# A gated recurrence: root of 1 - a^2 rewritten with a tanh of the half, its square on GpSimd removed

## The chip, the core and the metric

One core of a Trainium2 chip runs one program. Its engines have a queue of instructions each: TensorE (PE, matmuls), VectorE (DVE), ScalarE (ACT), GpSimd (POOL) and SyncE (SP, which issues transfers). The time is the device time of one execution in microseconds (us); the kernel before took 2144.94 us, the median of three runs (2142.59 to 2145.22).

## What is computed

One block of a diffusion model over 2048 tokens of 1024 features. A token mixer has three branches: a gated linear recurrence in both directions over 512 features, a pooling branch and a gated MLP; a feed-forward part with a 3x3 convolution follows and takes most of the time. The change is in the coefficients of the recurrence:

```python
r = sigmoid(block_diag(xh, w_a, b_a))
i = sigmoid(block_diag(xh, w_x, b_x))
log_a = -LRU_C * r * softplus(-lam)
a = exp(log_a)
bterm = sqrt(-expm1(2.0 * log_a)) * (i * xf)
# then h[t] = a[t] * h[t-1] + bterm[t], forwards and backwards
```

The factor of `i * xf` is the root of 1 - a^2.

## The kernel before, in words

The features of the recurrence are four tiles of 128 (`j`), the tokens four chunks of 512 (`n`), and there are two directions (`d`). A unit (`lru_units`, written `f` or `b` in the list `ORDER`) works on one direction, one chunk and two tiles `j`; there are 8 forward units and then 8 backward ones. Ahead of them two context groups (`lru_ctx`, `c`) run the same steps on 256 context tokens, for two `j` and both directions at once, to give the first states.

A unit runs these steps for each of its two `j`. `coeffs` (L451): two matmuls into PSUM give the gates, then ScalarE takes the sigmoid of both (tiles `r` and `i`) and `t = tanh(k * r)`, where `k` is a column of `klam`, -8 times a softplus computed once by `lam_consts`; this tanh is that of log a itself. `coeffs2` (L465): ScalarE overwrites `r` by `a = exp(k * r)`; then `combine` (L471) lets GpSimd compute the square `q = r * r` (L473) and `i = i * xa` (L474), and VectorE the sum-and-product `t = (q + 1) * t` (L475). With tanh(x) = (e^2x - 1) / (e^2x + 1) that is a^2 - 1. `coeffs3` (L477): ScalarE takes the root of -t, and `finish_b` (L483) has GpSimd multiply `i` by it (L485). `scan` (L487, L491) is one VectorE instruction along the tokens; then the last state is kept (L526), and the result goes to memory (forwards) or is added to the forward result by GpSimd (`join`, L535).

All activations of ScalarE that need a table go through `act` (line 135 in the profile). It counts sigmoid and tanh as one set of functions, exp, sqrt, gelu and silu as sets of their own, and makes every instruction of a set follow those of the set before in the order of the program; a table is loaded at each change of set. So a unit has three loads: sigmoid and tanh, exp, sqrt. Other activations (identity, copy, square) may stand anywhere.

The tiles of a unit come from a pool of two (`lru_tile`), so a unit's sigmoids wait until the unit before has given its tile back. Beside the units, the same stretch of the program holds the matmuls of the input projection (`xa`, `gt`, `pl`, `uv`), the gating MLP (`gmlp`: L629 to L647, with `guv` on VectorE, `sp` and `tp` on TensorE), the pooling branch (`pool_br`: L561 to L592, with `pz`, `pa`, `pb` on VectorE and `pp` on TensorE), the modulation vectors (L672, VectorE) and the preparation of weights (L153, L271, L272, VectorE). `ORDER` gives the order in which these pieces are written; the order within each engine's queue is planned from it when the program is built, by priority and estimated durations, and each queue then runs strictly in that order. The stretch ends where the output projection starts (`wo`), at about 544 us. The feed-forward part (L376 to L378 `up`, L1023 and L1066 to L1068) follows to the end.

Of the kernel before, what the change touches and what calls it, by code (L numbers as in the profile page):

```python
# [11 lines left out]
AF = mybir.ActivationFunctionType  # L12
OP = mybir.AluOpType
# [4 lines left out]
LC = 256  # L18
CH = 512
# [49 lines left out]
def block_kernel(ctx: ExitStack, tc: tile.TileContext, x, xT, ctx_d, ctxT, cc, crow, cols_d, wm01, bm01, wmT,  # L69
                 win, wuv, gw, pw, wsT, gnorm, wout, wup, wdn, ident_d, out):  # L70
    nc = tc.nc
    V, A, G, T, S = nc.vector, nc.scalar, nc.gpsimd, nc.tensor, nc.sync
# [16 lines left out]
    def bank(tag, name):  # L89
        return banks["open"].tile([128, CH], F32, tag=tag, bufs=banks[tag], name=name)  # L90
# [24 lines left out]
    def col(name, i=0, n=1):  # L115
        return cols[:, OFF[name] + i:OFF[name] + i + n]
# [16 lines left out]
    def act(out_, in_, func, **kw):  # L133

        ins = A.activation(out_, in_, func, **kw).ins  # L135
        if SETS[func] != runs["set"]:
            runs.update(set=SETS[func], prev=runs["cur"], cur=[])
        for p in runs["prev"]:
            tc.add_manual_dep(ins, p.name, mybir.DependencyInfo(
                mybir.DependencyClass.NoSync, mybir.DependencyReason.DATA), reason="table set")  # L140
        runs["cur"].append(ins)
# [26 lines left out]
    Y = [ymix.tile([128, 4, CH], F32, name=f"Y{n}") for n in range(2)]  # L168
# [7 lines left out]
    def lru_tile(shape, dt, name):  # L176
        return mix.tile(shape, dt, tag="lru", bufs=2, name=name)
# [220 lines left out]
    klam = const.tile([128, 8], F32, name="klam")  # L398

    def lam_consts():  # L400
        e = small.tile([128, 8], F32, tag="l0", bufs=1, name="lam_e")
        y = small.tile([128, 8], F32, tag="l1", bufs=1, name="lam_y")
        y2 = small.tile([128, 8], F32, tag="l2", bufs=1, name="lam_y2")
        p = small.tile([128, 8], F32, tag="l3", bufs=1, name="lam_p")
        lam = col("lam", 0, 8)
        base = small.tile([128, 8], F32, tag="l4", bufs=1, name="lam_b")
        V.memset(base, 2.718281828459045)
        V.tensor_scalar(y, lam, -1.0, None, op0=OP.mult)
        V.tensor_tensor(e, lam, y, op=OP.min)
        G.tensor_tensor(e, base, e, op=OP.pow)  # L410
        V.tensor_scalar(y, e, 2.0, None, op0=OP.add)
        V.reciprocal(y, y)
        V.tensor_tensor(y, e, y, op=OP.mult)
        V.tensor_tensor(y2, y, y, op=OP.mult)
        V.tensor_scalar(p, y2, 1.0 / 17, 1.0 / 15, op0=OP.mult, op1=OP.add)
        for d in (13, 11, 9, 7, 5, 3, 1):
            V.tensor_tensor(p, p, y2, op=OP.mult)
            V.tensor_scalar(p, p, 1.0 / d, None, op0=OP.add)
        V.scalar_tensor_tensor(p, p, 2.0, y, op0=OP.mult, op1=OP.mult)
        V.tensor_scalar(y, lam, -1.0, 0.0, op0=OP.mult, op1=OP.max)  # L420
        V.tensor_tensor(p, p, y, op=OP.add)
        V.tensor_scalar(klam, p, -8.0, None, op0=OP.mult)


    halo = const.tile([128, 4, 2], F32, name="halo")
# [24 lines left out]
    state = const.tile([128, 4, 2], F32, name="state")  # L450

    def coeffs(j, d, xa, w, c=None, bank=None):
        bank = pB if bank is None else bank
        rp, ip = bank("rp"), bank("ip")
        T.matmul(rp[:, :w], gwt[:, j, 2 * d, :], xa, start=True, stop=True)  # L455
        T.matmul(ip[:, :w], gwt[:, j, 2 * d + 1, :], xa, start=True, stop=True)
        c = lru_tile([128, 4, CH], F32, "lru") if c is None else c
        r, i, t, q = (c[:, a, :] for a in range(4))
        act(r[:, :w], rp[:, :w], AF.Sigmoid, bias=col("ba", 4 * d + j))
        act(i[:, :w], ip[:, :w], AF.Sigmoid, bias=col("bx", 4 * d + j))  # L460
        k = klam[:, 4 * d + j:4 * d + j + 1]
        act(t[:, :w], r[:, :w], AF.Tanh, scale=k)
        return r, i, t, q, k

    def coeffs2(cs, xas, w):  # L465
        for c in cs:
            act(c[0][:, :w], c[0][:, :w], AF.Exp, scale=c[4])
        for c, xa in zip(cs, xas):
            combine(c, xa, w)

    def combine(c, xa, w):  # L471
        r, i, t, q, k = c
        G.tensor_tensor(q[:, :w], r[:, :w], r[:, :w], op=OP.mult)  # L473
        G.tensor_tensor(i[:, :w], i[:, :w], xa, op=OP.mult)  # L474
        V.scalar_tensor_tensor(t[:, :w], q[:, :w], 1.0, t[:, :w], op0=OP.add, op1=OP.mult)  # L475

    def coeffs3(cs, w):  # L477
        for c in cs:
            act(c[2][:, :w], c[2][:, :w], AF.Sqrt, scale=-1.0)
        for c in cs:  # L480
            finish_b(c, w)

    def finish_b(c, w):  # L483
        i, t = c[1], c[2]
        G.tensor_tensor(i[:, :w], i[:, :w], t[:, :w], op=OP.mult)  # L485

    def scan(o, c, w, init, rev):  # L487
        r, i = c[0][:, :w], c[1][:, :w]
        if rev:
            o, r, i = o[:, ::-1], r[:, ::-1], i[:, ::-1]  # L490
        V.tensor_tensor_scan(o, r, i, init, op0=OP.mult, op1=OP.add)  # L491

    xac = []
# [10 lines left out]
    def lru_ctx(js):  # L504
        jd = [(j, d) for j in js for d in range(2)]
        ts = [lru_tile([128, 4, CH], F32, "lrc") for j in js]
        cs = [coeffs(j, d, xac[0][:, j, :], LC, ts[j - js[0]][:, :, d * LC:(d + 1) * LC]) for j, d in jd]
        coeffs2(cs, [xac[0][:, j, :] for j, d in jd], LC)
        coeffs3(cs, LC)
        for (j, d), c in zip(jd, cs):  # L510
            q = c[3]
            scan(q, c, LC, 0.0, d == 1)
            e = LC - 1 if d == 0 else 0
            V.tensor_copy(state[:, j, d:d + 1], q[:, e:e + 1])
# [2 lines left out]

    def lru_units(d, n, js, sink):
        cs = [coeffs(j, d, Y[n][:, j, :], CH, bank=b) for j, b in zip(js, (pB, pA))]
        coeffs2(cs, [Y[n][:, j, :] for j in js], CH)  # L520
        coeffs3(cs, CH)
        for j, c in zip(js, cs):
            o = c[3]
            scan(o, c, CH, state[:, j, d:d + 1], d == 1)
            e = CH - 1 if d == 0 else 0
            V.tensor_copy(state[:, j, d:d + 1], o[:, e:e + 1])  # L526
            sink(j, n, o)
# [9 lines left out]
    def fwd(n, js):  # L537
        lru_units(0, n, js, keep_f)

    def bwd(n, js):  # L540
        lru_units(1, n, js, join)
# [198 lines left out]
    prep_uv([conv0])  # L740
    set_inv(10)
    lam_consts()

    def xstats(n):
# [29 lines left out]
    def preps():  # L774
# [8 lines left out]
    run = {  # L783
        "x": lambda n: xnext(int(n)),
        "c": lambda j: lru_ctx(J[j]),
        "a": lambda n, j: xa(int(n), J[j]),
        "f": lambda n, j: fwd(int(n), J[j]),
# [155 lines left out]
    for i in range(len(tiles) + 2):  # L943
        if i < len(tiles):
            n, tt = tiles[i]
# [165 lines left out]
    for c in range(NP + 1):  # L1111
        if c < NP:
            gi, i = divmod(c, GRP)
# [11 lines left out]
        for s in range(8):  # L1125
# [10 lines left out]
            if s % 4 == 3 and c > 0 and c % GRP == 0:  # L1136
                q = s // 4
# [108 lines left out]
```

## Time and profile before

| | |
|---|---|
| median of three runs | 2144.94 us |
| profiled execution | 2143.54 us |
| its span, first to last instruction | 2141.8 us |
| TensorE busy | 2006.3 us (94%) |
| VectorE busy | 1586.2 us (74%) |
| ScalarE busy | 1194.2 us (56%) |
| GpSimd busy | 611.9 us (29%) |
| mean granted TensorE clock | 0.969 |
| table loads on ScalarE | 77, 98.8 us |

The busy shares are averages over the whole span, most of which is the feed-forward part. A row of the timeline gives the start, the duration and the instruction with its tiles (output<-inputs) and shapes; in brackets stands how long the engine had been idle before it and what ended that. "x2" in a timeline are two instructions in a row, with the time from the start of the first to the end of the last. A row of the waits says who waited for whom: total, number of times, longest. All ScalarE activations with a table have the helper's line, L135.

### The profile page before, as it was taken

The page shows a single profiled execution, that of the slowest core. Times are in us where ns is not written, and L with a number is a line of the kernel's source. Part 1 is how long each engine was busy: PE and PEld are TensorE (multiplying, and loading weights), DVE is VectorE, ACT ScalarE, POOL GpSimd, SP SyncE. Part 2 cuts the span into 40 slices and gives each one's busy share as a digit, 9 for nine tenths or more (in the row PEclk, how much of TensorE's full clock was granted, in tenths as well). Part 3 has the DMA queues.
Part 4 walks back from the last instruction along what each step waited for, and adds up shares of the span by engine and source line. Part 5 has one row for each costly group of instructions (what it writes and reads, how often), then busy time and mean ns, then how long its engine had stood idle before and what let it go on. Part 6 is the DMA issues. An engine that isn't in the chain of part 4 may idle for free.

```text
span 2141.8 us, 24253 instructions
## 1 busy us (share of the span) xinstructions
PE 2006.3 (94%) x9203; PEld 930.4 (43%) x9203; DVE 1586.2 (74%) x2212; ACT 1194.2 (56%) x1665; POOL 611.9 (29%) x457
## 2 busy tenths in 40 slices
PE   5878989798899998999999999999999999999995
PEld 1433444343455543444444444444444444444442
DVE  5787778999565259978767776867777686777876
ACT  4776755455255446656565555645556465555453
POOL 2332334445256411101121121112212121221156
PEclk8989999899999999999999999999999999999998
DMA  8421243412333110315455464545545454454238
GB/s 339 181 99 47 69 153 113 158 40 93 134 133 128 60 64 20 138 68 124 89 122 95 79 132 73 101 83 104 90 88 106 71 103 88 101 94 68 40 157 157
DMA packets 74564, 225.03 MB, mean 105 GB/s; under 512 B 8400, under 2 KB 19024, under 8 KB 69584
## 3 DMA queue, kind: packets, MB, share of 16 engines
q0 software_dynamic: 21312, 77.60, 21.5%
q1 hardware_dynamic: 53136, 145.89, 19.7%
q8 instruction: 72, 1.18, 0.2%
q14 instruction: 44, 0.36, 0.1%
HBM read 120.70 MB, written 102.76 MB: 104 GB/s over the span
## 4 chain that ended last, share of the span: by engine, by line
PE 54%; DVE 5%; POOL 1%; ACT 1%; issue 1%; DMA 0%; POOLq 0%; SPq 0%; DVEq 0%; ACTq 0%
PE up L376 12%; PE up L378 12%; PE up L377 12%; PE dn L1066 6%; PE dn L1068 6%; PE dn L1067 6%; DVE cv L1023 3%; DVE hT L1098 0%; POOL hT L1081 0%; DVE hT L1072 0%; DMA wm<-in_wmT_dram 0%; DVE g L1031 0%; POOL fms L159 0%; PE sct L121 0%; POOL out_dram L1099 0%
## 5 line engine op out<-in xcount | busy, mean ns | idle before, releaser
L1023 DVE SCALAR_TENSOR_TENSOR cv<-z,cols,cv 128x1008 f32<-128x1008 f32 (+3 forms) x704 | 870.4, 1250 | 274.8 <-ACT cv L1017 187.0
L376 PE MATMUL up<-hT,uw 128*128 128x512 f16 x1408 | 534.3, 379 | 2.4 <-ACT z L858 2.4
L377 PE MATMUL up<-hT,uw 128*128 128x512 f16 x1408 | 534.2, 379 | 0.0
L378 PE MATMUL up<-hT,uw 128*128 128x512 f16 x1408 | 534.1, 379 | 0.0
L1083 POOL DMA_DIRECT2D accd<-dd x132 | 114.2, 865 | 701.0 <-ACT dd L1077 694.8
L858 ACT ACTIVATE z<-up,upinv 128x512 f32<-128x512 f32 x176 | 120.5, 684 | 308.9 <-PE up L378 308.5
L1077 ACT ACTIVATE dd<-dn,gdi 128x512 f32<-128x512 f32 x320 | 214.1, 680 | 112.9 <-PE dn L1068 106.4
L1066 PE MATMUL dn<-dw,gs 128*128 128x512 f16 x704 | 266.6, 379 | 5.4 <-ACT dd L1077 3.6
L1067 PE MATMUL dn<-dw,gs 128*128 128x512 f16 x704 | 266.7, 379 | 0.0
L1068 PE MATMUL dn<-dw,gs 128*128 128x512 f16 x704 | 265.1, 379 | 0.0
L376 PEld LDWEIGHTS <-uw 128*128 128x128 f16 x1408 | 139.1, 99 | 164.5 <-issue 0.6
L377 PEld LDWEIGHTS <-uw 128*128 128x128 f16 x1408 | 137.9, 98 | 167.2 <-issue 3.4
L378 PEld LDWEIGHTS <-uw 128*128 128x128 f16 x1408 | 137.9, 98 | 166.6 <-issue 0.8
L844 POOL TENSOR_TENSOR uw<-ur,uw 128x2048 f16<-128x2048 f32 x22 | 89.5, 4069 | 169.2 <-ACT ur L843 169.2
L135 ACT ACT_TABLE_LOAD x77 | 98.8, 1283 | 53.8 <-PE rp L455 24.2
L1017 ACT ACTIVATE cv<-z,cols 128x1024 f32<-128x1024 f32 x88 | 106.0, 1206 | 2.0
L1066 PEld LDWEIGHTS <-gs 128*128 128x128 f16 x704 | 72.1, 102 | 78.3
L1067 PEld LDWEIGHTS <-gs 128*128 128x128 f16 x704 | 68.7, 98 | 84.7 <-issue 7.0
L1068 PEld LDWEIGHTS <-gs 128*128 128x128 f16 x704 | 68.8, 98 | 83.1
L998 POOL TENSOR_TENSOR dw<-dr,dw 128x1024 f16<-128x1024 f32 x22 | 46.5, 2128 | 141.8 <-PE dn L1068 100.4
L150 ACT ACTIVATE junk<-g 128x1024 bf16<-128x1024 f32 x44 | 46.3, 1053 | 58.9 <-DVE g L1031 58.8
L890 PE MATMUL wo<-wo,ysp 128*128 128x512 f16 x256 | 77.6, 385 | 1.0 <-ACT gm L819 1.0
(303 smaller groups left out, 3052.9 us busy)
## 6 DMA issues: line engine op xcount, KB each, us to landing
accd<-dd POOLq DMA_DIRECT2D x132, 512.0 KB, 5.1
ur<-in_wup_dram SPq DMA_DIRECT2D x22, 1024.0 KB, 5.5
wm<-in_wmT_dram SPq DMA_DIRECT2D x64, 256.0 KB, 2.9
dr<-in_wdn_dram SPq DMA_DIRECT2D x22, 512.0 KB, 4.8
hT<-in_wm_dram SPq DMA_DIRECT2D x8, 1024.0 KB, 11.7
xt<-in_xT_dram SPq DMA_DIRECT2D x8, 1024.0 KB, 7.1
ro<-in_wout_dram SPq DMA_DIRECT2D x16, 512.0 KB, 3.5
xr<-in_x_dram SPq DMA_DIRECT2D x16, 512.0 KB, 3.7
```

The lines of the kernel that those rows point to most:

```text
L135: ins = A.activation(out_, in_, func, **kw).ins
L376: T.matmul(ps, wh(k), hh(k), start=(k == 0), stop=False)
L377: T.matmul(ps, wh(k), hl(k), start=False, stop=False)
L378: T.matmul(ps, wl(k), hh(k), start=False, stop=(k == KT - 1))
L858: A.activation(z[:, ab, b * 8:(b + 1) * 8, :], ps.rearrange("p (r x) -> p r x", x=64), AF.Identity, scale=upinv[:, c:c + 1])
L1017: A.activation(t, z[:, ab, r0:r0 + 16, :].rearrange("p r x -> p (r x)"), AF.Identity, bias=col("fcb", c + NP * ab), scale=wt(0, 0))
L1023: V.scalar_tensor_tensor(o, z[:, ab, ya + dy:yb + dy, xa + dx:xb + dx], wt(dy, dx), o, op0=OP.mult, op1=OP.add)
L1066: T.matmul(ps[h], hi, wh, start=i == 0, stop=False)
L1067: T.matmul(ps[h], hi, wl, start=False, stop=False)
L1068: T.matmul(ps[h], lo, wh, start=False, stop=i == n - 1)
L1077: A.activation(d[:, h * CH:(h + 1) * CH], ps[h], AF.Copy, scale=di)
L1083: G.dma_start(accd[t], d, accum_op=OP.add)
```

## The change

The square root is taken of another term. With tanh(x/2) = (a - 1) / (a + 1) for x = log a, (1 + a) times the root of -tanh(x/2) is the root of (1 + a)^2 (1 - a) / (1 + a), which is the root of 1 - a^2. So the tanh is taken with half the factor (-4 instead of -8 times the softplus; the new constants overwrite the columns `lam` of the table `cols`), the root no longer needs the exponential and is issued straight behind it on ScalarE, GpSimd's square is gone, and VectorE's sum-and-product now reads the exponential and the root and stands between the root and GpSimd's last product. Both products of GpSimd stay; the scan writes into the same tile as before.

```diff
--- before.py
+++ after.py
@@ -420,6 +420,7 @@
         V.tensor_scalar(y, lam, -1.0, 0.0, op0=OP.mult, op1=OP.max)
         V.tensor_tensor(p, p, y, op=OP.add)
         V.tensor_scalar(klam, p, -8.0, None, op0=OP.mult)
+        V.tensor_scalar(lam, p, -4.0, None, op0=OP.mult)
 
 
     halo = const.tile([128, 4, 2], F32, name="halo")
@@ -450,42 +451,30 @@
     state = const.tile([128, 4, 2], F32, name="state")
 
     def coeffs(j, d, xa, w, c=None, bank=None):
+
         bank = pB if bank is None else bank
         rp, ip = bank("rp"), bank("ip")
         T.matmul(rp[:, :w], gwt[:, j, 2 * d, :], xa, start=True, stop=True)
         T.matmul(ip[:, :w], gwt[:, j, 2 * d + 1, :], xa, start=True, stop=True)
         c = lru_tile([128, 4, CH], F32, "lru") if c is None else c
-        r, i, t, q = (c[:, a, :] for a in range(4))
-        act(r[:, :w], rp[:, :w], AF.Sigmoid, bias=col("ba", 4 * d + j))
-        act(i[:, :w], ip[:, :w], AF.Sigmoid, bias=col("bx", 4 * d + j))
-        k = klam[:, 4 * d + j:4 * d + j + 1]
-        act(t[:, :w], r[:, :w], AF.Tanh, scale=k)
-        return r, i, t, q, k
-
-    def coeffs2(cs, xas, w):
-        for c in cs:
-            act(c[0][:, :w], c[0][:, :w], AF.Exp, scale=c[4])
-        for c, xa in zip(cs, xas):
-            combine(c, xa, w)
-
-    def combine(c, xa, w):
-        r, i, t, q, k = c
-        G.tensor_tensor(q[:, :w], r[:, :w], r[:, :w], op=OP.mult)
-        G.tensor_tensor(i[:, :w], i[:, :w], xa, op=OP.mult)
-        V.scalar_tensor_tensor(t[:, :w], q[:, :w], 1.0, t[:, :w], op0=OP.add, op1=OP.mult)
-
-    def coeffs3(cs, w):
-        for c in cs:
-            act(c[2][:, :w], c[2][:, :w], AF.Sqrt, scale=-1.0)
-        for c in cs:
-            finish_b(c, w)
-
-    def finish_b(c, w):
-        i, t = c[1], c[2]
-        G.tensor_tensor(i[:, :w], i[:, :w], t[:, :w], op=OP.mult)
+        r, i, t, q = (c[:, a, :w] for a in range(4))
+        act(r, rp[:, :w], AF.Sigmoid, bias=col("ba", 4 * d + j))
+        act(i, ip[:, :w], AF.Sigmoid, bias=col("bx", 4 * d + j))
+        act(t, r, AF.Tanh, scale=col("lam", 4 * d + j))
+        return r, i, t, q, klam[:, 4 * d + j:4 * d + j + 1]
+
+    def coeffs2(cs, xas):
+        for r, i, t, q, k in cs:
+            act(r, r, AF.Exp, scale=k)
+        for r, i, t, q, k in cs:
+            act(t, t, AF.Sqrt, scale=-1.0)
+        for (r, i, t, q, k), xa in zip(cs, xas):
+            G.tensor_tensor(i, i, xa, op=OP.mult)
+            V.scalar_tensor_tensor(q, r, 1.0, t, op0=OP.add, op1=OP.mult)
+            G.tensor_tensor(i, i, q, op=OP.mult)
 
     def scan(o, c, w, init, rev):
-        r, i = c[0][:, :w], c[1][:, :w]
+        r, i = c[0], c[1]
         if rev:
             o, r, i = o[:, ::-1], r[:, ::-1], i[:, ::-1]
         V.tensor_tensor_scan(o, r, i, init, op0=OP.mult, op1=OP.add)
@@ -505,8 +494,7 @@
         jd = [(j, d) for j in js for d in range(2)]
         ts = [lru_tile([128, 4, CH], F32, "lrc") for j in js]
         cs = [coeffs(j, d, xac[0][:, j, :], LC, ts[j - js[0]][:, :, d * LC:(d + 1) * LC]) for j, d in jd]
-        coeffs2(cs, [xac[0][:, j, :] for j, d in jd], LC)
-        coeffs3(cs, LC)
+        coeffs2(cs, [xac[0][:, j, :] for j, d in jd])
         for (j, d), c in zip(jd, cs):
             q = c[3]
             scan(q, c, LC, 0.0, d == 1)
@@ -517,8 +505,7 @@
 
     def lru_units(d, n, js, sink):
         cs = [coeffs(j, d, Y[n][:, j, :], CH, bank=b) for j, b in zip(js, (pB, pA))]
-        coeffs2(cs, [Y[n][:, j, :] for j in js], CH)
-        coeffs3(cs, CH)
+        coeffs2(cs, [Y[n][:, j, :] for j in js])
         for j, c in zip(js, cs):
             o = c[3]
             scan(o, c, CH, state[:, j, d:d + 1], d == 1)
```

## Rows read from the trace of the kernel before

**Rows 1.** Three stretches: busy PE, PEld, DVE, ACT, POOL; clock, DMA.
```profile
85.00:345.00 260.00, 224.04 (x935) 106.64 (x935) 203.64 (x401) 181.59 (x263) 100.18 (x96) 0.93 0.25 87
345.00:540.00 195.00, 162.69 (x620) 71.00 (x617) 183.20 (x308) 92.52 (x117) 86.97 (x58) 0.90 0.35 110
560.00:2141.00 1581.00, 1546.48 (x7292) 717.74 (x7289) 1131.84 (x1310) 868.90 (x1198) 407.47 (x288) 0.99 0.43 96
```

**Rows 2.** Waits from 345 to 540 us: us in total, times, longest.
```profile
ACT lru L135 <- DVE lru L475: 27.6, 10, 6.6
PE pp L547 <- DVE pb L586: 15.9, 5, 5.4
```

**Rows 3.** Instructions on tile lru: shortest/median/longest ns, starts.
```profile
L473 POOL TENSOR_TENSOR lru<-lru x32: 1034/1086/2017, 148.8 to 518.8; 128x512 f32<-128x512 f32 x32
L475 DVE SCALAR_TENSOR_TENSOR lru<-lru x32: 673/684/1747, 151.5 to 520.3; 128x512 f32<-128x512 f32 x32
L135 ACT ACTIVATE lru<-lru x32: 612/630/632, 152.2 to 521.0; 128x512 f32<-128x512 f32 x32
```

**Rows 4.** Timeline of GpSimd and VectorE at 372 us: start, us, instruction.
```profile
371.91 3.45 POOL L473 TENSOR_TENSOR lru<-lru 128x512 f32<-128x512 f32 x2 [0.65 <-ACT lru L135]
...
372.41 2.06 DVE L153 SCALAR_TENSOR_TENSOR ro<-ro 128x1024 f32<-128x1024 f32 x1
375.97 1.21 DVE L153 SCALAR_TENSOR_TENSOR ro<-ro 128x1024 f32<-128x1024 f32 x1
```

**Rows 5.** Timeline of ScalarE and VectorE, the unit at 452 us.
```profile
450.38 1.28 ACT L135 ACT_TABLE_LOAD   x1
451.68 1.33 ACT L135 ACTIVATE lru<-lru,klam 128x512 f32<-128x512 f32 x2
453.02 1.28 ACT L135 ACT_TABLE_LOAD   x1
455.09 0.63 ACT L135 ACTIVATE lru<-lru 128x512 f32<-128x512 f32 x1 [0.78 <-DVE lru L475]
...
453.55 1.51 DVE L475 SCALAR_TENSOR_TENSOR lru<-lru 128x512 f32<-128x512 f32 x1 [1.60 <-POOL lru L473]
```

**Rows 6.** Timeline of ScalarE and VectorE, the units at 475 and 518 us.
```profile
474.93 1.28 ACT L135 ACT_TABLE_LOAD   x1
...
475.60 2.11 DVE L475 SCALAR_TENSOR_TENSOR lru<-lru 128x512 f32<-128x512 f32 x2
...
518.35 1.28 ACT L135 ACT_TABLE_LOAD   x1
...
518.87 2.11 DVE L475 SCALAR_TENSOR_TENSOR lru<-lru 128x512 f32<-128x512 f32 x2
```

**Rows 7.** Timeline of ScalarE and VectorE, the unit at 378 us.
```profile
372.47 1.28 ACT L135 ACT_TABLE_LOAD   x1
379.05 1.23 ACT L135 ACTIVATE lru<-lru 128x512 f32<-128x512 f32 x2 [5.30 <-DVE lru L475]
...
378.33 1.28 DVE L475 SCALAR_TENSOR_TENSOR lru<-lru 128x512 f32<-128x512 f32 x2
```

**Rows 8.** Groups from 85 to 345 us: busy us, mean ns, idle before, releaser.
```profile
L475 DVE SCALAR_TENSOR_TENSOR lru<-lru 128x512 f32<-128x512 f32 x18 | 19.3, 1101 | 23.9 <-POOL lru L473 23.9
```

**Rows 9.** Timeline of ScalarE and VectorE, the units at 199 and 240 us.
```profile
198.98 1.28 ACT L135 ACT_TABLE_LOAD   x1
...
198.83 1.51 DVE L475 SCALAR_TENSOR_TENSOR lru<-lru 128x512 f32<-128x512 f32 x1 [7.28 <-POOL lru L473]
...
239.28 1.28 ACT L135 ACT_TABLE_LOAD   x1
...
239.80 2.11 DVE L475 SCALAR_TENSOR_TENSOR lru<-lru 128x512 f32<-128x512 f32 x2 [5.93 <-POOL lru L473]
```

**Rows 10.** Timeline of TensorE, its wait at 204 us.
```profile
204.10 0.41 PE L644 MATMUL tp<-ident,guv 128*128 128x128 f32 x2 [3.71 <-DVE guv L642]
```

**Rows 11.** Timeline of VectorE, the scan at 505 us.
```profile
505.36 1.28 DVE L491 TENSOR_TENSOR_SCAN lru<-lru,state 128x512 f32<-128x512 f32 x1 [1.17 <-POOL lru L485]
```

## The prediction

> **What bounds the kernel now.** I read the stretches first [rows 1]. From 560 us on TensorE is busy 1546.48 of 1581 us; the change issues nothing there, so that part can only be shifted. What the change touches lies between 85 and 540 us, and this falls into two halves. Up to 345 us TensorE is busy 224 of 260 us and VectorE 204: neither is full, and they take turns in holding the other. From 345 to 540 us VectorE is busy 183.20 of 195 us, TensorE 162.69, ScalarE only 92.52, GpSimd 86.97: VectorE's queue sets the pace. The waits of that half say the same [rows 2]: TensorE waits 15.9 us for `pb`, a VectorE result. ScalarE waits 27.6 us for L475, the largest wait of the half and the one that the change takes away outright; but ScalarE is idle half of the time there, so these 27.6 us are mostly not on the path. What counts is what the change does to VectorE's time and to the places where VectorE or TensorE stands still.
>
> **GpSimd's square (L473) goes.** There are 32 on 128x512 elements, 1.086 us by the median [rows 3], and 8 half as wide in the context groups. GpSimd's own time is hardly needed, but a square slows VectorE while both run. In the unit at 372 us two squares cover 371.91 to 375.36 us; beside them a 128x1024 sum of squares takes 2.06 us, and the same instruction just after them 1.21 [rows 4]: 0.85 us lost to VectorE beside less than two squares. In the backward half I compared each VectorE instruction that lies mainly under a square with the quickest of its kind: twelve are longer, from the first at 372.41 us (0.85 us, [rows 4]) to the last at 518.87 us (0.83 us: 2.11 us for the pair of L475 against 1.28 at 378.33 us, [rows 6, 7]), each by 0.68 to 0.86 us, 9.8 us in all. **Term 1: -9.8 us** of VectorE in the half where VectorE is full. It can't be more than the own time of the half's fourteen squares, 15.2 us at the median [rows 3], nor can it fall below zero unless the products (L485) take over the squares' place, which is the no-change rival.
>
> **The sum-and-product (L475) now waits for ScalarE's root instead of GpSimd's square.** This is the added wait, and it is longer when ScalarE is on time. In the unit at 452 us the two exponentials end at 453.01, the table load runs from 453.02 to 454.30, and the root then waits 0.78 us for L475 [rows 5]. Afterwards the root starts at 454.31, takes 0.63 [rows 3], and L475 can start at about 455.0; before, the first square let it start at 453.55 [rows 5]. The delay is 1.45 us. Behind it on VectorE stands the pooling branch, for whose result TensorE waits [rows 2]. In the units at 475 and 518 us the load ends at 476.21 and 519.63; adding the root's 0.63, L475 starts at 476.9 and 520.3 where it started at 475.60 and 518.87 [rows 6]: delays of 1.3 and 1.45 us. In the other four units of that half VectorE gets to L475 so late that ScalarE waits for it (5.30 us in the unit where the load had ended at 373.75, [rows 7]; 6.6 at the most, [rows 2]); there the root is ready and no wait arises. **Term 2: +4.2 us.**
>
> In the forward half six of the nine main units have VectorE idle before L475 already, 23.9 us in all [rows 8], but mostly while TensorE has matmuls of its own. Two units have the gating MLP's L641 and L642 behind L475, and TensorE behind those. At 198.83 us the load ends at 200.26, so L475 starts at 200.95, 2.1 us later [rows 9]; it then takes 0.68 us [rows 3] instead of 1.51, since no square runs beside it, so what follows is 1.3 us later, and TensorE's wait of 3.71 us for `tp` grows by that [rows 10]. At 239.80 us the same reckoning (load over at 240.56, L475 at 241.2, [rows 9]) gives 1.4 - 0.83 = 0.6 us. **Term 3: +1.9 us.** In the other units of the forward half I put both the delay and the shorter L475 (18 times 1.101 against 0.684 us, 7.5 us, [rows 3, 8]) at nothing, because TensorE covers them; without that cover they could cost 0.6 us each or, where VectorE isn't waiting, give back 0.8 each.
>
> **The root leaves the way from L475 to the scan.** Before: L475, root 0.63 us, product, scan. Now the product follows L475 directly. Where VectorE is behind, the product starts earlier by at least the root's 0.63 us [rows 3]; between 378 and 380 us L475 and root follow each other in that way [rows 7]. Only one scan of the second half waits for its product, 1.17 us at 505.36 [rows 11]; it gains 0.6 and the other scans stand in VectorE's queue anyway. **Term 4: -0.6 us.** In an undisturbed unit the scan starts at the same time as now: the root ends one load and 0.63 us behind the exponential, and L475's 0.68 us takes the place of the wait of 0.78 us.
>
> **Small edits.** The new constant is one VectorE instruction on 128x8 elements: nothing, since it comes with the other constants, well before the first unit; not covered it costs at most the 0.673 us of the quickest L475 on 512 columns [rows 3]. It writes into the table of columns, so readers of that table may have to wait for it, by no more than the same. The tanh reads another column at the same price. The root has the same 32 + 8 instructions and the same table loads; no DMA and no matmul changes, and the queues of DMA issues are passed by nothing.
>
> **A rule against it.** Between the exponentials and the root lies a change of table; the load's row is 1.28 us, and the exponentials behind the one at 450.38 start 0.02 us after its end [rows 5]. The Trainium skill (ScalarE: Activation LUTs, "What ACT_TABLE_LOAD costs") puts a switch at 1283 ns for the load and about 1380 ns more for a drain, 2.66 us in all. By that, an estimate from that page, each of the five delays above would be 1.38 us longer and the sum would come to about +2.6 us, no change. No row here shows such a drain: ScalarE idles 0.02 us before the second load there too, so the sum keeps the load's row.
>
> **Sum.** -9.8 + 4.2 + 1.9 - 0.6 = -4.3 us. The profiled execution took 2143.54 us (its span and 1.74 us around it), so it would come to 2139.2; the median of the runs is 1.4 us higher, 2144.94, which gives **2140.6 us**. A measurement of this kernel can tell about 0.2%, 4.3 us, from nothing, so the forecast lies just at that bound.
>
> **The rivals.** (a) *Larger gain.* The order in each queue is planned when the program is built, and the plan can move other VectorE work ahead of L475; then terms 2 and 3 don't arise and TensorE's 3.71 us at 204.10 [rows 10] go too: -9.8 - 0.6 - 3.7 = -14.1 us, 2130.8 us. For it: in four of seven units of the second half L475 is late already. Against: in the first half it wasn't planned so.
> (b) *No change.* VectorE, being quicker, reaches L475 early in all seven units of the second half and waits 1.4 us in each, 9.8 us, which eats term 1; with terms 3 and 4 that is 2146.2 us. A switch of tables that takes longer than its load's row would end here too; against [rows 5] that has little of this chance.
> (c) *Slower.* In the forward half L475 is planned to the head of VectorE's queue with the gating MLP behind it in all nine units and the two context groups: 11 waits of 1.4 us are 15.4 us, less the 7.5 us of shorter L475, +7.9 us; the second half is even as in (b): 2152.8 us. It decides from about six such units on (two now have TensorE behind them). For it: 23.9 us of idle time before L475 show that the plan takes its input to be ready sooner than it is, and the load now lies ahead of it as well. Against: TensorE has work of its own under most.
> (d) That the change doesn't do what it says would need a plan in which an activation of another table gets between exponential and root; line 135 orders the sets, so I leave it 1 in 100, within (c).
>
> **Chances.** Forecast 0.42 (its own range 2136 to 2144.5: 0.25 beyond the bound of 0.2%, 0.17 within it), (a) 0.20, (b) 0.15, (c) 0.23. Faster: 0.25 + 0.20 = 0.45; the same: 0.17 + 0.15 = 0.32; slower: 0.23. The range takes in (a) with some of term 1's open end, and nearly all of (c): 2127 to 2152 us.
>
> **What would show it.** In the profile after: no L473, 40 roots that wait for nothing, POOL less busy by some 35 us for the 32 large squares (1.086 us each, [rows 3]) and a few for the small ones. Right if VectorE's busy time between 345 us and the start of the output projection falls by about 10 us, while its waits for ScalarE's root come to a few us there. (b) shows as waits of 1.4 us before every L475; (c) as longer waits of TensorE for `tp` before 345 us; (a) as neither. Wrong altogether if the part behind the output projection changes its own length by more than 2 us.

## The result, and the profile after

The changed kernel takes 2155.72 us (median of four runs, 2154.08 to 2158.72) against 2143.77 us of the kernel before beside it: a ratio of 1.0057 [1.0043, 1.0071] (in brackets here and below the 95% interval). It is slower by 12 us, where -4.3 us was forecast, and lies above the range. The profiled execution took 2154.9 us, its span is 2153.1 us.

The first rows of the output projection and of the feed-forward part, in the timeline of TensorE, tell where the time was lost. The kernel before:

```profile
544.04 1.01 PE L890 MATMUL wo<-wo,ysp 128*128 128x512 f16 x2 [1.05 <-ACT gm L819]
...
725.15 0.38 PE L376 MATMUL up<-hT,uw 128*128 128x512 f16 x1
```

The changed kernel:

```profile
555.17 1.01 PE L877 MATMUL wo<-wo,ysp 128*128 128x512 f16 x2 [1.08 <-ACT gm L806]
...
735.27 0.38 PE L376 MATMUL up<-hT,uw 128*128 128x512 f16 x1
```

The projection starts 11.1 us later, the feed-forward part 10.1, and the whole span is 11.3 us longer (2153.1 against 2141.8): nearly all of it is lost ahead of the projection, where the recurrence is. The stretches that answer to [rows 1] (busy PE, PEld, DVE, ACT, POOL; clock, DMA):

```profile
85.00:345.00 260.00, 212.88 (x878) 100.71 (x878) 187.21 (x394) 172.90 (x252) 73.55 (x66) 0.91 0.26 87
345.00:540.00 195.00, 165.28 (x633) 72.50 (x632) 170.05 (x292) 99.69 (x128) 75.55 (x47) 0.91 0.31 100
560.00:2141.00 1581.00, 1557.76 (x7338) 722.59 (x7336) 1135.82 (x1318) 872.10 (x1204) 406.09 (x287) 1.00 0.43 96
```

GpSimd is relieved as forecast: 575.3 us busy in all instead of 611.9. VectorE is busy 16.4 us less up to 345 us and 13.2 less from there to 540 us, and yet it is later. Part of the 13.2 is work that has only moved behind 540 us: up to the start of the projection VectorE is busy 187.2 us before (345 to 544 us) and 184.2 after (345 to 555 us), 3.0 less. The instructions on the tile `lru`, beside [rows 3] (the line numbers moved: the sum-and-product is L473 now, GpSimd's last product L474):

```profile
L135 ACT ACTIVATE lru<-lru x32: 612/623/632, 158.6 to 531.4; 128x512 f32<-128x512 f32 x32
L473 DVE SCALAR_TENSOR_TENSOR lru<-lru x32: 675/685/1757, 159.3 to 532.2; 128x512 f32<-128x512 f32 x32
L474 POOL TENSOR_TENSOR lru<-lru x32: 1257/1583/2249, 160.1 to 534.0; 128x512 f32<-128x512 f32 x32
```

The first unit's sum-and-product starts at 159.3 us instead of 151.5. Where VectorE's time went instead is in the groups, from 85 to 345 us (beside [rows 8]) and from 345 to 565 us; behind the bar stand busy time, mean, and idle time before:

```profile
L473 DVE SCALAR_TENSOR_TENSOR lru<-lru 128x512 f32<-128x512 f32 x16 | 13.8, 887 | 32.1 <-ACT lru L135 32.1
...
L473 DVE SCALAR_TENSOR_TENSOR lru<-lru 128x512 f32<-128x512 f32 x16 | 10.5, 685 | 20.5 <-ACT lru L135 20.5
```

VectorE stands 52.6 us before the sum-and-product, where before it stood 25.5 (7 waits, 23.9 us of them in [rows 8]). The kernel before, from 85 to 545 us:

```profile
L475 DVE SCALAR_TENSOR_TENSOR lru<-lru 128x512 f32<-128x512 f32 x32 | 31.9, 1022 | 25.5 <-POOL lru L473 25.5
```

The same is seen in one unit, in the timeline of ScalarE and VectorE that answers to [rows 5]:

```profile
456.77 1.28 ACT L135 ACT_TABLE_LOAD   x1
458.07 1.33 ACT L135 ACTIVATE lru<-lru,klam 128x512 f32<-128x512 f32 x2
459.41 1.28 ACT L135 ACT_TABLE_LOAD   x1
460.70 1.15 ACT L135 ACTIVATE lru<-lru 128x512 f32<-128x512 f32 x2
...
461.43 1.29 DVE L473 SCALAR_TENSOR_TENSOR lru<-lru 128x512 f32<-128x512 f32 x2 [3.09 <-ACT lru L135]
```

The two exponentials end at 459.40, and 2.03 us later VectorE starts: load, one root, the hand-over. In [rows 5] it started 0.54 us after the exponentials' end. But there is a second difference, which no row of one instruction shows: with another graph of instructions the plan made at the build came out differently. The table below sets each engine's queue up to the output projection beside that of the kernel before, as lists of the same instructions.

| queue | instructions | in another place |
|---|---|---|
| VectorE | 805 | 411 |
| TensorE | 1677 | 254 |
| ScalarE | 352 | 57 |
| SyncE | 173 | 38 |
| GpSimd | 125 | 9 |

Most instructions have moved by a few places, some of VectorE's and TensorE's by about twenty. The new constant has no part in it: added alone to the kernel before, it leaves all five queues as they were.

### The profile page after: what moved, and what is told of

Its sections match the earlier page's. It is cut to its first block, busy times and chain, and to the rows that moved or that the text cites. A ratio compares the mean times of both kernels' runs of the same rounds, so it can differ in the third digit from the quotient of the medians.

```text
span 2153.1 us, 24225 instructions
## 1 busy us (share of the span) xinstructions
PE 2005.5 (93%) x9203; PEld 930.6 (43%) x9203; DVE 1566.8 (73%) x2213; ACT 1193.7 (55%) x1665; POOL 575.3 (27%) x417
## 4 chain that ended last, share of the span: by engine, by line
PE 55%; DVE 3%; POOL 1%; issue 1%; DMA 1%; ACT 1%; POOLq 0%; SPq 0%; DVEq 0%; ACTq 0%
PE up L376 12%; PE up L378 12%; PE up L377 12%; PE dn L1053 6%; PE dn L1055 6%; PE dn L1054 6%; DVE cv L1010 2%; DMA hT<-accd 1%; POOL hT L1068 0%; DVE hT L1085 0%; DVE hT L1059 0%; DMA wm<-in_wmT_dram 0%; POOL fms L159 0%; PE sct L121 0%; POOL out_dram L1086 0%
```

## The experiments

**Theories.** W: the wait for the root costs the 12 us, since a table load now stands between exponential and sum-and-product. P: the plan's other order costs them. To separate the two, the order of the queues was taken out of the plan's hands:

```diff
     close_psum()
+    force(nc, tc)
...
+def force(nc, tc):
...
+        for p, q in zip(o, o[1:]):
+            tc.add_manual_dep(emitted[e][q], emitted[e][p].name, mybir.DependencyInfo(
+                mybir.DependencyClass.NoSync, mybir.DependencyReason.DATA), reason="fixed order")
```

`o` is a list written into the kernel, one for each engine, of all instructions ahead of the output projection; each is tied to the one before it, without a semaphore. So any arithmetic can be run in any order that it allows. Tied to its own order, either kernel comes out as the same program, instruction for instruction, so the ties themselves cost nothing. All ratios below are against the kernel before on the same chip, whose medians in the three sets of runs were 2142.76, 2142.42 and 2142.99 us.

### Arithmetic and order exchanged

**e1_ab**, the changed arithmetic in the order of the kernel before:

> The changed arithmetic with every engine's queue, up to the output projection, pinned to the order of the kernel before (the squares drop out, the new constant stands behind the old one). If the wait for the root costs the 12 us by itself (theory W), the order does not matter and this runs at about 2156 us, 10 to 14 above the kernel before. If the plan's other order costs them (theory P), it runs within 4 us of the kernel before, 2140 to 2147.

Measured: 2143.10 us, ratio 1.0005 [0.9995, 1.0015]. As P has it: in the old order the same arithmetic, with its waits for the root, costs nothing measurable.

**e2_ba**, the old arithmetic in the changed kernel's order. The squares have no place in that order; in GpSimd's queue they were put right ahead of each group's first final product (L485), behind the products with `xa`.

> The arithmetic of the kernel before, squares and all, with the queues pinned to the order of the changed kernel (each group's squares ahead of its first product). Theory P: about 2156 us, 10 to 14 above the kernel before. Theory W: within 3 us of it.

Measured: 2161.25 us, ratio 1.0088 [1.0073, 1.0103]: 18.5 us more, and more than P had. How much of that is the squares' late place was not separated. W has none of it.

### The loads taken away

The root's activation was made an exponential, so that it needs no change of table:

```diff
     def act(out_, in_, func, **kw):
...
-        ins = A.activation(out_, in_, func, **kw).ins
+        ins = A.activation(out_, in_, AF.Exp if func == AF.Sqrt else func, **kw).ins
```

This takes 18 of the 77 loads, one in each of 16 units and two context groups. **e3_an**, in the changed kernel's own order:

> The changed kernel in its own order, the root's activation replaced by an exponential of the same shape, so that no table is loaded between exponential and root (left out: the root's values). Theory W: the sum-and-product no longer waits for the load, VectorE's idle time ahead of it falls from some 52 us to under 25 us, and the time falls by 10 us or more, to 2146 or less. Theory P: the wait at 150 us and the others of the order stay, and the time falls by less than 6 us, to above 2150.

Measured: 2141.13 us, ratio 0.9993 [0.9983, 1.0002], 14.6 us less than the changed kernel. That is W's figure, though e1 had just spoken for P. W missed the idle time: it falls to 37.4 us, not under 25. Three waits of VectorE in the timeline tell why. The changed kernel:

```profile
208.21 1.29 DVE L473 SCALAR_TENSOR_TENSOR lru<-lru 128x512 f32<-128x512 f32 x2 [8.63 <-ACT lru L135]
...
328.09 0.69 DVE L473 SCALAR_TENSOR_TENSOR lru<-lru 128x512 f32<-128x512 f32 x1 [3.41 <-ACT lru L135]
...
351.13 1.29 DVE L473 SCALAR_TENSOR_TENSOR lru<-lru 128x512 f32<-128x512 f32 x2 [7.97 <-ACT lru L135]
```

The same three without the load (e3_an):

```profile
200.94 1.29 DVE L473 SCALAR_TENSOR_TENSOR lru<-lru 128x512 f32<-128x512 f32 x2 [7.21 <-ACT lru L135]
...
319.18 0.69 DVE L473 SCALAR_TENSOR_TENSOR lru<-lru 128x512 f32<-128x512 f32 x1 [2.00 <-ACT lru L135]
...
340.81 1.29 DVE L473 SCALAR_TENSOR_TENSOR lru<-lru 128x512 f32<-128x512 f32 x2 [6.55 <-ACT lru L135]
```

Each wait is 1.41 or 1.42 us shorter, one load and its hand-over, and no more; the rest of it is the unit's own chain of activations. That holds for six of VectorE's ten waits before the sum; the other four differ by between 0.2 us more and 5.0 us less. The 14.6 us are ten times one such wait.

**e4_bn**, the same in the kernel before:

> The same replacement in the kernel before, in its own order (left out: the root's values): what the two loads of each root are worth where the sum-and-product stands ahead of the root. Both theories: little, 2 to 5 us below the kernel before, because only the state waits for them there; the difference between this and the changed kernel without its root is then what is left of the change without loads.

Measured: 2143.02 us, ratio 0.9998 [0.9988, 1.0007]: nothing by the median, less than the little that was expected. There the load lay beside the square and the sum-and-product, as [rows 5] show. In the one trace the projection does start 4.0 us sooner, at 540.06 us, and the feed-forward part then takes 3.0 us longer, so the load was covered but for 0 to 4 us. The 18 loads are gone from ScalarE here as well, so ScalarE's time by itself is not what costs 14.6 us in e3.

**e8_abn**, the changed arithmetic without the loads in the order of the kernel before:

> The changed arithmetic in the order of the kernel before (2143.1 us as measured), the root's activation replaced by an exponential so that no table is loaded between exponential and root (left out: the root's values). If the load lies on the path in any order, 2130 to 2134, as the 14.6 us that it took in the changed kernel's own order. If the order of the kernel before has work over it, 2139 to 2143.

Measured: 2128.86 us, ratio 0.9935 [0.9920, 0.9949]. On the path in the old order too. The loss builds up from unit to unit: in e1 the first sigmoids start 2.7 us later than in e8 in the first unit, 9.3 us in the ninth, the last one that starts up to 345 us, and the projection 16.0. The medians in one table (us; they are from different sets, between which the kernel before varied by 1.4 us):

| | old order | changed kernel's order |
|---|---|---|
| arithmetic of before | 2142.76 | 2161.25 |
| the same, no load before the root | 2143.02 | |
| changed arithmetic | 2143.10 | 2155.72 |
| the same, no load before the root | 2128.86 | 2141.13 |

Down the first column: the changed arithmetic is worth 14.2 us where no load stands in it, and the load takes 14.2 back. Across: the order adds 12.6 us with the loads and 12.3 without. So the 12 us against the kernel before are the order's, as P has it. W fails as it was put (e1 was to run at about 2156 us), but the load does cost some 14 us; the rest of the change gains as much and pays for it.

The start of the projection in the traces, one execution of each, says the same with other sizes. e1, e8 and e4:

```profile
545.38 1.01 PE L877 MATMUL wo<-wo,ysp 128*128 128x512 f16 x2 [1.05 <-ACT gm L806]
...
529.35 1.01 PE L877 MATMUL wo<-wo,ysp 128*128 128x512 f16 x2 [1.05 <-ACT gm L806]
...
540.06 1.01 PE L890 MATMUL wo<-wo,ysp 128*128 128x512 f16 x2 [1.05 <-ACT gm L819]
```

There the order is worth 9.8 us (to 555.17 in the changed kernel), the load 16.0 and the rest of the change 10.7. The feed-forward part, in which no run changes anything, takes from 1416.1 us (e1) to 1419.7 us (e11) in the traces. A difference of some 3 us between two kernels is therefore not to be read closely.

### Where the order costs

The queues of the two orders hold exactly the same instructions up to about 188 us and up to about 370 us, so they can be joined there. Three kernels have the changed kernel's order in one of the three stretches and the old order in the others.

**e5_order_early**

> The changed arithmetic; queues in the changed kernel's own order up to about 188 us (context groups and the first forward unit) and in the order of the kernel before from there to the output projection. If the loss sits at the wait of 15.9 us at 150 us and its neighbours, this runs at about 2150 to 2156. If it is spread, or lies later, 2143 to 2148.

Measured: 2147.90 us, ratio 1.0021 [1.0012, 1.0031], 4.8 us above e1.

**e6_order_mid**

> The same with the changed kernel's own order only from about 188 to 370 us (the other forward units and the first backward one). Spread: 2146 to 2150. All of it here: 2155.

Measured: 2150.21 us, ratio 1.0039 [1.0025, 1.0053], 7.1 us above e1.

**e7_order_late**

> The same with its own order only from about 370 us to the output projection (backward units and pooling branch). Spread: 2146 to 2150. All of it here: 2155. If the three losses add up, their sum is the 12.6 us between the pinned order of the kernel before and the changed kernel.

Measured: 2149.02 us, ratio 1.0031 [1.0019, 1.0043], 5.9 us above e1. The loss is spread. The three come to 17.8 us, more than the 12.6 together; with an interval of 2 to 3 us to either side of each that excess is hardly clear of noise, and whether a later stretch hides part of what an earlier one lost was not shown.

In two of the stretches the traces show one place each where a step arises; neither exchange was made alone. In e1 the second unit's first sigmoid starts 35.1 us after the first one's (143.8, 178.9), in e5 38.7 (145.1, 183.8); from there on the shift stays between 4.2 and 6.9 us up to the last unit, and 3.1 us of it are left at the projection. The rows ahead of it in e5 (timeline of VectorE, then TensorE):

```profile
145.03 4.39 DVE L267 SCALAR_TENSOR_TENSOR hT<-xt,gsl,hT 128x512 f16<-128x512 f32 x5
149.34 0.74 DVE L432 SCALAR_TENSOR_TENSOR Y<-xa,cwz,Y 128x511 f32<-128x511 f32 x1
...
150.79 0.14 DVE L502 COPY state<-lrc 128x1 f32<-128x1 f32 x1
...
150.92 2.08 PE L457 MATMUL rp<-Y,gwt 128*128 128x512 f32 x2 [15.97 <-DVE state L502]
```

and in e1:

```profile
145.91 0.14 DVE L502 COPY state<-lrc 128x1 f32<-128x1 f32 x1
145.97 4.40 DVE L267 SCALAR_TENSOR_TENSOR hT<-xt,gsl,hT 128x512 f16<-128x512 f32 x5
...
146.04 2.07 PE L457 MATMUL rp<-Y,gwt 128*128 128x512 f32 x2 [3.31 <-DVE state L502]
```

The five instructions of L267, which prepare the next chunk of tokens, stand ahead of the convolution and the state copy in the one order and behind them in the other; behind that exchange TensorE's gate matmuls start 4.9 us later. In e6 the step lies between the eighth and the ninth unit: 22.4 us (315.5, 337.9) instead of 16.4 (317.7, 334.1). The timeline of TensorE in e6:

```profile
331.71 1.13 PE L622 MATMUL sp<-guv,wst 128*128 128x128 f32 x8 [1.74 <-DVE guv L617]
...
335.49 1.02 PE L457 MATMUL rp<-Y,gwt 128*128 128x512 f32 x2
```

and in e1:

```profile
330.96 1.02 PE L457 MATMUL rp<-Y,gwt 128*128 128x512 f32 x2
...
334.61 1.06 PE L622 MATMUL sp<-guv,wst 128*128 128x128 f32 x8
```

The gate matmuls of the ninth unit stand behind the gating MLP's matmuls, which wait for VectorE themselves, instead of ahead of them. Of this step only 1.8 us are left at the projection of that trace (547.21 us), and 3.3 us of its longer span lie in the feed-forward part, so the 7.1 us of the median are not explained by it. In e7 the shift against e1 swings from unit to unit, between 0.4 and 9.7 us, and 5.4 us are left at the output projection; no single exchange was made out there, and that stays open.

### Held queue or long chain

The load costs 14 us in either order, but it may do so in two ways at once: VectorE's queue is held, and each unit's chain to its scan is longer. To tell them apart the sum was moved to the end: GpSimd multiplies by the root, and VectorE's sum-and-product stands right ahead of its scan.

```diff
-        for (r, i, t, q, k), xa in zip(cs, xas):
-            G.tensor_tensor(i, i, xa, op=OP.mult)
-            V.scalar_tensor_tensor(q, r, 1.0, t, op0=OP.add, op1=OP.mult)
-            G.tensor_tensor(i, i, q, op=OP.mult)
+        for r, i, t, q, k in cs:
+            G.tensor_tensor(i, i, t, op=OP.mult)
+        for r, i, t, q, k in cs:
+            V.scalar_tensor_tensor(i, r, 1.0, i, op0=OP.add, op1=OP.mult)
```

The product with `xa` is written ahead of the exponentials. **e9_sum_last**, with the old order pinned (the sum moved to its scan):

> The changed arithmetic in the order of the kernel before (2143.1 us), but GpSimd multiplies i * xa by the root and VectorE's sum-and-product comes last, right ahead of its scan; exponential and root stay in their order on ScalarE, so each unit's chain is as long as before this edit, and VectorE's queue is no longer held early. If the 14.2 us of the loads are VectorE's queue standing behind the sum-and-product, most of them come back: 2129 to 2134. If they are the length of the unit's own chain, 2140 to 2145.

Measured: 2139.38 us, ratio 0.9984 [0.9974, 0.9994]: 3.7 us below e1, just below the second forecast. In the groups from 85 to 545 us e1 has

```profile
L473 DVE SCALAR_TENSOR_TENSOR lru<-lru 128x512 f32<-128x512 f32 x32 | 23.3, 748 | 45.9 <-ACT lru L135 45.9
L473 DVE SCALAR_TENSOR_TENSOR lrc<-lrc 128x256 f32<-128x256 f32 x8 | 4.1, 551 | 13.5 <-ACT lrc L135 13.5
```

and e9

```profile
L475 DVE SCALAR_TENSOR_TENSOR lru<-lru 128x512 f32<-128x512 f32 x32 | 35.6, 1113 | 22.7 <-POOL lru L473 22.7
...
L475 DVE SCALAR_TENSOR_TENSOR lrc<-lrc 128x256 f32<-128x256 f32 x8 | 4.6, 578 | 5.9 <-POOL lrc L473 5.9
...
L430 DVE SCALAR_TENSOR_TENSOR Y<-xa,cwz,Y 128x511 f32<-128x511 f32 x12 | 8.9, 742 | 16.1 <-ACT Y L429 16.1
```

VectorE's idle time before the sum fell from 59.4 to 28.6 us, by 30.8, and the time by 3.7 (the start of the projection by 7.6 in the traces). Most of the idle time was not saved but moved: 16.1 us now stand before the convolution (L430), which had none in e1, and from 85 us to the projection VectorE is idle 87.6 us in e1 and 78.2 in e9. The sum itself also takes longer (1113 ns instead of 748 in the mean), but VectorE's whole busy time up to the projection hardly differs, 372.7 and 374.6 us. That speaks for the chain as the larger part.

**e10_root_first** has the roots ahead of the exponentials as well:

```diff
+        for (r, i, t, q, k), xa in zip(cs, xas):
+            G.tensor_tensor(i, i, xa, op=OP.mult)
+            act(t, t, AF.Sqrt, scale=-1.0)
+        for (r, i, t, q, k), xa in zip(cs, xas):
+            G.tensor_tensor(i, i, t, op=OP.mult)
+            act(r, r, AF.Exp, scale=k)
```

> As the run before, and the roots stand ahead of the exponentials on ScalarE: GpSimd's product then runs beside the exponential's load, and the chain of a unit is shorter by one GpSimd product, some 1.3 us and a hand-over. Held queue: as the run before, 2129 to 2134. Length of the chain: 1.3 to 2 us less in each of some ten units, 2124 to 2131.

Measured: 2127.14 us, ratio 0.9927 [0.9912, 0.9942], 12.2 us below e9 (8.9 at the start of the projection in the traces, e9's being its fastest execution and e10's its slowest), as the chain's length has it. In its timeline (ScalarE, GpSimd, VectorE) a unit looks like this:

```profile
230.36 1.15 ACT L135 ACTIVATE lru<-lru 128x512 f32<-128x512 f32 x2
231.53 1.28 ACT L135 ACT_TABLE_LOAD   x1
232.82 1.33 ACT L135 ACTIVATE lru<-lru,klam 128x512 f32<-128x512 f32 x2
...
231.13 2.69 POOL L471 TENSOR_TENSOR lru<-lru 128x512 f32<-128x512 f32 x2 [1.23 <-ACT lru L135]
...
234.03 0.68 DVE L474 SCALAR_TENSOR_TENSOR lru<-lru 128x512 f32<-128x512 f32 x1
234.74 1.28 DVE L480 TENSOR_TENSOR_SCAN lru<-lru,state 128x512 f32<-128x512 f32 x1
```

GpSimd's products, 231.13 to 233.82, lie beside the load and the exponentials, 231.53 to 234.15; sum and scan follow without a gap. VectorE's idle time before the sum falls too, from 28.6 to 11.7 us, so e10 alone does not separate the two readings; that it is the chain rests on e9 and e10 together. This version leaves nothing out and beats both kernels: 15.9 us below the kernel before, 28.6 below the changed one.

**e11_sum_last_own_plan** and **e12_root_first_own_plan** are the same two edits with the order that was planned for them:

> The edit with the sum last, with the order that is planned for it at the build. If the order found for the changed kernel was one unlucky draw, this lies within 4 us of the pinned version; if the planner does badly on every graph in which root and exponential stand side by side, 8 us or more above it.

> The edit with the roots first and the sum last, with the order that is planned for it at the build. The same two cases: within 4 us of its pinned version, or 8 us or more above it.

Measured: 2145.49 us, ratio 1.0010 [1.0000, 1.0019], 6.1 us above e9, between the two cases; and 2139.48 us, ratio 0.9979 [0.9970, 0.9989], 12.3 us above e10. With the changed kernel that is three graphs out of three whose own plan is 6 to 13 us worse than the order inherited from the kernel before. Why the plans come out worse was not looked into.

## Why the prediction was wrong

**The sum was reckoned in queues that the change did not keep.** This is the step that failed. The text said that the order is planned at the build, but let a new plan come up only in the rivals, as a gain in (a) and as more waits for the root in (c); every term of the sum moved instructions within the queues of before. In those queues the forecast was not far off, -4.3 us against +0.3 in e1, but that was luck: it set 10.4 us of gain against 6.1 of loss, and measured were some 14 on either side. The other 12.6 us are the new order's, and no term had them. The trace of before could not show that order; that the plan itself is a cost of unknown sign belonged in the range. The text's own sign failed as well: VectorE's busy time between 345 us and the projection was to fall by about 10 us and fell by 3.0, and the waits for the root there were to be a few us and are 20.5.

**Term 1** (-9.8 us, squares that slow VectorE): too small, and looked for in one half only. Without loads the changed arithmetic is worth 14.2 us (e4 to e8). This holds two things that were not separated: VectorE no longer slowed, and a chain shorter by one square. In e1 the sum-and-products alone take 23.3 us against the 31.9 of before. But VectorE's busy time between 345 us and the output projection fell by 5.5 us only (187.2 to 181.7), not by about 10, and by 13.0 ahead of 345 us (203.64 to 190.68), where the text had put the shorter instructions at nothing. Reckoned as in the text, each VectorE instruction under a large square against the quickest of its kind, twelve in the forward half lose 9.3 us, as twelve in the backward half lose 9.8; the text counted the second half alone. In e1 both are gone, but by an estimate of the same kind some 3 us come back in the backward half, beside GpSimd's products and its additions in `join`.

**Terms 2 and 3** (+4.2 and +1.9 us): that the load delays the sum was right, and the size of one wait too (1.3 to 1.45 us forecast, 1.41 measured), but five units were counted. The load costs 14.2 us, ten times 1.41. The second step that failed is the sentence that TensorE covers the other units of the forward half: of what e1 loses against e8, 9.3 us are there at the ninth unit. The sentence was argued from who waits next in the queue, and e9 makes that the smaller part, 3.7 us. What each load lengthens, as e9 and e10 suggest, is the unit's chain, and the next unit's sigmoids and TensorE's gate matmuls come behind its end.

**Term 4** (-0.6 us) lies within that chain and was not measured alone. Nor were the small edits; the new constant does not move the plan. The signs of the change itself came: no L473, 40 roots that wait for nothing, GpSimd busy 36.6 us less.

**The rule against it.** A load and a drain of 2.66 us in each change of table (the Trainium skill, ScalarE: Activation LUTs, "What ACT_TABLE_LOAD costs") would have made the waits of e3 and of the changed kernel differ by that much. The three that are shown differ by 1.41 or 1.42 us, so the row of the load was the right price. By the Trainium skill's figure the sum was +2.6 us, nearer to the result, but not for its reason.

**The rivals.** (a) had the new plan, with the wrong sign. (b), no change, is what e1 measures, +0.3 us against its kernel before where (b) had +1.3, but by larger terms on both sides. (c) comes nearest to the result, 2152.8 against 2155.72 us, and has the longer waits in more units; but its waits were to decide the forward half by themselves, and e1 has them in all nine units and both context groups and loses nothing over the whole: the gain of the rest of the change pays for them. Nor did its sign come: up to 345 us TensorE waits 11.7 us for `tp` in the changed kernel and 15.6 before. (d) did not arise: in each unit the roots follow right behind the load.

## What to carry to other kernels

An edit that changes the graph of a kernel with planned queues is two changes, the arithmetic and the new order; pin the old order once and run both, before a word is said on the arithmetic. That the queues differ can be seen ahead of any run, by laying the two plans side by side. Count an added wait by the length of the chain in which it stands, per repetition, and not by who is next in the waiting engine's queue: 30.8 us of idle time less before one instruction were worth 3.7 us, one product moved beside a load in each unit 12.2. Where two changes of table lie in a chain, put the function first whose result another engine still has work for, as e10 does.

## What was not expected of the hardware

After TensorE's wait of 15.94 us in the changed kernel the granted clock is 0.50 from 153.0 to 155.5 us, that is 1.2 GHz, and the 128x512 matmuls that follow take 0.63 us; from 156 us on it is 1.00, and they take 0.38. In e1 a wait of 3.31 us stands in that place, and the clock in the 2.5 us from 149.0 is 0.94, a mean over both levels. So this wait cost a little more than its length: the first five of these matmuls start over 2.05 us, where five of the later ones take 1.08. From 85 us to the start of the projection the mean clock is 0.91 in the changed kernel and in e1, so the clock is not what sets the two apart.
